# Gathering the small products of several streams in bursts, and FoX's stages at another place, in a one-core hybrid RWKV-7/FoX decoder block

## The chip, the cores and the metric

The kernel runs on one core of a Trainium2 chip. The core has a matrix engine (TensorE; PE in the profile, its weight loads PEld), a vector engine (VectorE, DVE), a scalar engine (ScalarE, ACT), GpSimd (POOL) and SyncE (SP), whose queue issues nearly all transfers. Each engine works through its own instructions in the order in which they were written for it, and waits on semaphores for the others. The metric is the time of one execution on the device in microseconds; the median of three runs is used.

## The reference

One decoder block over 16 meta tokens and 256 tokens (272 columns), width 2048, in float32. What is computed, cut to what matters:

```python
xn = _rms(h, n1)
z_rwkv, z_fox, z_gate = jnp.split(xn @ w_in, ...)          # 6608 + 4096 columns of w_in
z_rwkv = z_rwkv + (z_prev - z_rwkv) * mu                   # token shift
y_a = _rwkv7(z_rwkv, ...)    # scan over tokens: S = S*w + (S a) b + v k ; y = S r, 16 heads of 64
y_b = _fox(z_fox, ...)       # causal softmax attention with a forget bias, 16 heads of 64
merged = sigmoid(g_a) * (y_a @ w_a) + sigmoid(g_b) * (y_b @ w_b)
h = h + merged @ w_o
gate, up = jnp.split(_rms(h, n2) @ w_gu, 2, axis=-1)
out = h + (silu(gate) * up) @ w_dn
```

## The kernel before

**Weight products.** Every weight matrix streams through SBUF in blocks of 128x1024 (`wload`, L313 to L318): SP requests `raw`, ACT rounds it to `wh`, DVE forms the rest `wl = raw - wh`, three buffers of each. A job (`cm_jobs`) is one block: 24 products of about 260 columns (k, v, r, most of f), or 16 products for f's queries and the gates zg, alternating 512 and 256 columns. They are in a float32 form that PE takes in one pass, and they are the bulk of PE's work.

**Streams.** The RWKV and FoX work is done in four groups of four heads. For each group the weight products k, v, r, then f (queries, keys, values) are followed by gate jobs zg. What comes after a projection is written as Python generators ("streams"): `rwkv_bg` (the RWKV part of a group), `sums`/`norms` and `fox_bg` (FoX), `forget_gate`, `lerp`'s second half. Each piece of a stream up to a `yield` is a stage; a stage mostly has some small fp32 products on PE (`pe_mm`, L350), or transposes (`pe_tr`, L354), and reads of their results by ACT and DVE. The value that it yields is the least distance to its next stage, in ns.

**What sets the order.** PE's order is the order in which the program is written. `slot(ns)` is called after each few weight products; it adds their length to a clock, and if stages are due, it writes the one with the earliest due time there, and then lets `max(GAP, MIX * cost)` of weight products go by. So each stage stands alone between two weight products. The order on the other engines, and of SP's requests, is set by the framework's own scheduler.

**Names.** In `rwkv_bg`: ss (head sums of squares), kx (spreading a norm back), mat and mat0 (the matrices of a chunk of 64 tokens), bs (bonus), trbk, trv, tr (transposes), then the triangular solve on DVE (lt, lx; the "lane"), whose result goes out and comes back as X through requests on SP (d, X), then per chunk rhs, then u and y, then s and y, and at the end yT. QT and X (32x32 products) belong to the solve. In FoX: fss, fx, pv and pvm (values transposed), and per pair of heads m = 0, 1: bias (one buffer, requested on SP from ncd), sc (scores), the softmax on DVE and ACT, ppt and ptm (transposes of the probabilities), pT and pM (their copies by ACT), po (the product with the values).

**Shapes.** PE is used as 128x128 by the weight products, the transposes, ss and fss; as 128x64 by rhs, s, the second part of y, and po; as 64x64 by u and the first part of y; as 64x128 by mat and sc; as 32x32 by QT and X. Results of stages go to four auxiliary PSUM banks in turn (`aux_ps`); the other four belong to the weight products.

Of the kernel before, what the change touches and what calls it, by code (L numbers as in the profile page):

```python
# [12 lines left out]
AF = mybir.ActivationFunctionType  # L13
# [49 lines left out]
LANE = 24000  # L63
GAP = 250
LERP = 2800
BIAS = 7000
STEP = 1000
# [7 lines left out]
X_DIV = 2600  # L75
X_PT = 1400
Y_SQ = 1400
# [7 lines left out]
Y_TRBK = 1400  # L85
Y_TRV = 1100
Y_TR0 = 1600
# [9 lines left out]
def hybrid_block(ctx, tc, A, out, dbg=None):  # L97
# [240 lines left out]

    def spawn(gen, delay):
        streams.append([clock[0] + delay, gen])  # L340

    def stage(st):
        try:
            st[0] = clock[0] + (next(st[1]) or HOP)
        except StopIteration:
            streams.remove(st)

    def pe_mm(out_, lhsT, rhs, start, stop, skip=False):
# [7 lines left out]
    def slot(ns):  # L356


        clock[0] += ns
        if clock[0] < clock[1]:  # L360
            return
        due = [st for st in streams if st[0] <= clock[0]]
        if due:
            clock[2] = 0.0
            stage(min(due, key=lambda st: st[0]))
            clock[1] = clock[0] + max(GAP, MIX * clock[2])

# [285 lines left out]
    def rwkv_bg(g, box):  # L653
# [15 lines left out]
        nc.scalar.activation(sq, kk, AF.Square)  # L669
        yield Y_SQ  # L670
        kn_ = rw.tile([P, 12], F32, tag="kn", name=f"kn{g}", bufs=2)
# [4 lines left out]
        backs = [spread(kr_, m, L, f"kx{g}{m}") for m in range(2)]  # L676
        yield Y_SPREAD
        for m in range(2):
# [37 lines left out]
        split(*parts, sq[:, :, :T])  # L716
        yield Y_AB

# [3 lines left out]
        for m in range(2):  # L722
            pss = [aux_ps(f"mat{g}{m}{h}") for h in range(2)]
            for c in range(4):
                for h in range(2):
                    pe_mm(pss[h][:, c * P:(c + 1) * P], bk[hb(h), m, c].rearrange("p x t -> p (x t)"),
                                     ar[hb(h), :, m, tok(c)], start=True, stop=True)
            for h in range(2):
                nc.vector.tensor_tensor(NK[:, h, 4 * m:4 * m + 4, :], pss[h].rearrange("p (c w) -> p c w", w=P),
                                        bcast(mup, 4), op=ALU.mult)  # L730
            yield Y_MAT
        pss = [aux_ps(f"mat0{g}{h}") for h in range(2)]
# [32 lines left out]
        yield Y_NEXT  # L765

        bo = ot(f"bo{g}")
        for m in range(2):
# [5 lines left out]
            nc.gpsimd.tensor_scalar(bo[:, m, :], bo[:, m, :], vi("gn_b", m), None, op0=ALU.add)  # L774
        yield Y_BONUS

# [5 lines left out]
        for m in range(2):  # L782
            ps = aux_ps(f"trbk{g}{m}")
            for c in range(4):
                pe_tr(ps[:, c * P:(c + 1) * P], bkf[:, 4 * m + c, :], ident)
            nc.scalar.activation(BK[:, :, 4 * m:4 * m + 4, :].rearrange("p h c d -> p c h d"),
                                 ps.rearrange("p (c h d) -> p c h d", h=2, d=HD), AF.Copy)
            yield Y_TRBK
        ps = aux_ps(f"trv{g}")
# [47 lines left out]
        def step(c, S, BK, SV, NK, X, Y):  # L837
# [24 lines left out]
            for h in range(2):  # L862
                nc.vector.tensor_copy(SV[0:nt, h, mine, :], pv2(ps)[h * HD:h * HD + nt])
            yield Y_U
            if not last:
# [20 lines left out]
            if not first:  # L886
                nc.scalar.activation(Y.rearrange("p (m c) v -> p m c v", m=2)[:, :, c, :], pv2(psy), AF.Copy)
            yield HOP

# [7 lines left out]
        next(meta_steps)  # L897
        yield Y_XT
        ps = aux_ps(f"QT{g}")
# [6 lines left out]
        next(meta_steps)  # L906
        yield Y_QT
        ps = aux_ps(f"X12{g}")
# [22 lines left out]
        nc.vector.tensor_tensor(Y, Y, s2.unsqueeze(2).to_broadcast([P, 8, HD]), op=ALU.mult)  # L931
        yield NORM
        ps = aux_ps(f"yT{g}")
# [28 lines left out]
    def fox_jobs(g):  # L962
# [18 lines left out]
        def norms():  # L981
            while len(done) < 2:
                yield
            yield from rsqrt_steps(fx, hr, hs, [P, 20], "ht")
            yield X_RS

            nc.vector.tensor_tensor(hs[:, 0:8], hs[:, 0:8], hr[:, 0:8], op=ALU.mult)
            backs = [spread(hr[:, 8:20], m, L, f"fx{g}{m}") for m in range(2)]
            yield X_SPREAD
            for m in range(2):  # L990
                nc.vector.tensor_tensor(kn[:, m, :], kn[:, m, :], backs[m](), op=ALU.mult)
            yield
            ready.append(1)

        def post(dst, n):
            def f(pss):
                sqs = []
                for m in range(2):
                    ps = pss[m]
                    if dst is vv:  # L1000
                        nc.scalar.activation(dst[:, m, :], ps[:, :n], AF.Copy)
                        continue
                    sq = fx.tile([P, L], F32, tag="sqf", name=f"sqf{g}", bufs=3)
                    if dst is qn:
                        halves(dst[:, m, :], ps)
                        nc.scalar.activation(sq[:, :n], dst[:, m, :], AF.Square)
                    else:
                        nc.scalar.activation(sq[:, :n], ps[:, :n], AF.Square)
                        nc.scalar.activation(dst[:, m, :], ps[:, :n], AF.Copy, scale=qk8)
                    sqs.append(sq)  # L1010
                if dst is vv:
                    spawn(fox_bg(g, qn, kn, vv, hs, hr, ready), HOP)
                else:
                    spawn(sums(sqs, dst, n), SUMS)
                    if dst is kn:
                        spawn(norms(), PREP)
            return f
# [4 lines left out]
    def fox_bg(g, qn, kn, vv, hs, hr, ready):  # L1022
# [18 lines left out]
        cmb = cmask.unsqueeze(1).to_broadcast([P, 2, P])  # L1041
        for m in range(2):

# [9 lines left out]
            nc.gpsimd.tensor_tensor(bias[:, :, d1], bias[:, :, d1], cmb, op=ALU.add)  # L1053
            yield BIAS
            sums = fx.tile([P, 4], F32, tag="sums", name=f"sums{g}{m}", bufs=2)

            nq = [NMETA + P, L]
            cq_ = [slice(0, nq[0]), slice(nq[0], nq[0] + nq[1])]
# [5 lines left out]
            for t in range(2):  # L1064
                n = nq[t]
                for h in range(2):
# [7 lines left out]
                    nc.scalar.activation(s[:, :n], s[:, :n], AF.Exp, scale=r, bias=nm,  # L1074
                                         accum_out=sums[:, 2 * t + h:2 * t + h + 1])
            yield X_SC + X_EXP
# [18 lines left out]
            nc.scalar.activation(pM[:NMETA], ptm[:NMETA, :2 * P].rearrange("p (h q) -> p h q", h=2)[:, :, 96:], AF.Copy)  # L1095
# [12 lines left out]
            nc.scalar.activation(yb[:, 2 * g + m, :], po[:, :T], AF.Copy)  # L1108
            yield

# [262 lines left out]
```

## Time and profile before

| | before |
|---|---|
| median of 3 runs | 1564.14 us (1563.58 to 1564.69) |
| profiled execution | 1564.61 us |
| its span, first to last instruction | 1562.9 us |
| PE busy in the span | 1554.3 us, 99% |
| DVE, ACT, POOL busy | 1016.3, 766.8, 103.5 us |
| share of PE in the chain that ended last | 95% |
| weight transfers and all others | 283.33 MB, mean 181 GB/s |

The stages stand in the first 607 us of the span; after that come the last gate jobs, the branches, w_o, the FFN. A row of the timeline gives the start and length in us, the engine and line, the operation, the tile written and those read, the array shape and the operand's columns, and how many instructions were merged; a bracket at the end says how long the engine was idle before it and what ended that. Matmuls overlap, so their lengths add up to more than the time; it is the distance from start to start that counts. An fp32 product shows as two matmul rows, so four products are x8.

### The profile page before, as it was taken

What the parts mean: (1) busy time and instruction counts of PE and PEld (TensorE: products, weight loads), DVE (VectorE), ACT (ScalarE), POOL (GpSimd) and SP (SyncE); (2) the same over time, 40 slices, a digit from 0 to 9 for tenths busy, and PEclk for the clock granted to TensorE, in tenths of its full rate; (3) what the DMA queues carried; (4) which work ended last, traced back from release to release, by engine and by line L of the source; (5) the groups of instructions that cost most, each with busy time, mean ns of one, the idle gap of its engine ahead of it and who ended that gap; (6) DMA issues with size and microseconds to landing.
All of it is one profiled execution on the core that took longest, in us unless ns stands there. A gap on an engine that the chain in (4) does not pass through costs nothing.

```text
span 1562.9 us, 26174 instructions
## 1 busy us (share of the span) xinstructions
PE 1554.3 (99%) x10227; PEld 1366.6 (87%) x10227; DVE 1016.3 (65%) x1854; ACT 766.8 (49%) x1117; POOL 103.5 (7%) x194
## 2 busy tenths in 40 slices
PE   9999999999999999999999999999999999999998
PEld 8999988989889888999888888888888888888887
DVE  8878688677768856875655666566566656444443
ACT  6655455465445544654444554454445544333332
POOL 2121103102203100000000000000000000000000
PEclk9999999999999999999999999999999999999999
DMA  7656546546545566776666666666666666666664
GB/s 238 177 155 173 158 125 180 157 119 168 166 137 146 166 179 190 248 226 225 190 183 181 186 186 190 189 188 188 189 189 188 185 193 187 187 203 198 188 200 131
DMA packets 211483, 283.33 MB, mean 181 GB/s; under 512 B 23888, under 2 KB 128352, under 8 KB 211360
## 3 DMA queue, kind: packets, MB, share of 16 engines
q1 hardware_dynamic: 206752, 277.43, 60.3%
q10 hardware_dynamic: 4608, 4.23, 0.8%
q8 instruction: 80, 1.31, 0.4%
q14 instruction: 43, 0.35, 0.1%
HBM read 274.43 MB, written 7.19 MB: 180 GB/s over the span
## 4 chain that ended last, share of the span: by engine, by line
PE 95%; DVE 2%; DMA 1%; issue 1%; ACT 1%; SPq 0%; ACTq 0%; DVEq 0%; POOL 0%
PE up L387 10%; PE gt L387 10%; PE zg L387 7%; PE dn L1238 5%; PE dn L1237 5%; PE dn L1236 5%; PE up L389 5%; PE gt L389 5%; PE zg L389 3%; PE f L328 2%; PE f L387 2%; PE f L330 2%; PE f L329 2%; PE br L329 2%; PE br L330 2%; PE br L328 2%
## 5 line engine op out<-in xcount | busy, mean ns | idle before, releaser
L318 DVE TENSOR_TENSOR wl<-raw,wh 128x1024 fp32r<-128x1024 f32 (+1 forms) x496 | 605.2, 1221 | 438.7 <-ACT wh L317 437.7
L317 ACT ACTIVATE wh<-raw 128x1024 fp32r<-128x1024 f32 (+1 forms) x496 | 521.3, 1052 | 628.7 <-PE dn L1237 146.3
L387 PE MATMUL gt<-hts,wh 128*128 128x512 f32 x704 | 245.0, 394 | 0.0
L387 PE MATMUL up<-hts,wh 128*128 128x512 f32 x704 | 244.9, 394 | 0.0
L389 PE MATMUL gt<-hts,wl 128*128 128x256 f32 x660 | 186.2, 282 | 0.0
L389 PE MATMUL up<-hts,wl 128*128 128x256 f32 x660 | 186.0, 282 | 0.0
L387 PE MATMUL zg<-xhl,wh 128*128 128x512 f32 x512 | 184.3, 403 | 0.0
L387 PEld LDWEIGHTS up<-hts,wh 128*128 128x128 f32 x704 | 130.1, 188 | 26.5
L387 PEld LDWEIGHTS gt<-hts,wh 128*128 128x128 f32 x704 | 130.1, 188 | 26.4
L1237 PE MATMUL dn<-wh,acl 128*128 128x512 f32 x352 | 139.5, 396 | 0.0
L1236 PE MATMUL dn<-wh,ach 128*128 128x512 f32 x352 | 139.5, 396 | 0.0
L1238 PE MATMUL dn<-wl,ach 128*128 128x512 f32 x352 | 139.5, 396 | 0.0
L389 PE MATMUL zg<-xhl,wl 128*128 128x256 f32 x480 | 135.0, 281 | 0.0
L389 PEld LDWEIGHTS up<-hts,wl 128*128 128x128 f32 x660 | 124.7, 189 | 1.8
L389 PEld LDWEIGHTS gt<-hts,wl 128*128 128x128 f32 x660 | 124.7, 189 | 1.8
L387 PEld LDWEIGHTS zg<-xhl,wh 128*128 128x128 f32 x512 | 94.6, 188 | 20.9 <-issue 1.8
L389 PEld LDWEIGHTS zg<-xhl,wl 128*128 128x128 f32 x480 | 90.6, 189 | 1.1
L1238 PEld LDWEIGHTS dn<-wl,ach 128*128 128x128 f32 x352 | 66.3, 188 | 16.2
L1237 PEld LDWEIGHTS dn<-wh,acl 128*128 128x128 f32 x352 | 66.3, 188 | 16.2
L1236 PEld LDWEIGHTS dn<-wh,ach 128*128 128x128 f32 x352 | 66.3, 188 | 16.1
L328 PE MATMUL f<-xhl,wh 128*128 128x272 f32 x256 | 77.7, 303 | 0.0
L330 PE MATMUL f<-xhl,wl 128*128 128x272 f32 x256 | 73.8, 288 | 0.0
(452 smaller groups left out, 2783.3 us busy)
## 6 DMA issues: line engine op xcount, KB each, us to landing
raw<-in_w_gate_up_dram SPq DMA_DIRECT2D x176, 512.0 KB, 3.8
raw<-in_w_in_dram SPq DMA_DIRECT2D x160, 512.0 KB, 4.1
raw<-in_w_down_dram SPq DMA_DIRECT2D x88, 512.0 KB, 4.7
raw<-in_w_o_dram SPq DMA_DIRECT2D x32, 512.0 KB, 4.3
raw<-in_w_branch_a_dram SPq DMA_DIRECT2D x16, 512.0 KB, 4.4
raw<-in_w_branch_b_dram SPq DMA_DIRECT2D x16, 512.0 KB, 4.8
zgd<-zg ACTq DMA_DIRECT2D x30, 128.0 KB, 2.4
gate<-zgd SPq DMA_DIRECT2D x15, 256.0 KB, 5.6
```

What stands on the lines that cost most here:

```text
L317: nc.scalar.activation(wh[:prow, cs_], raw[:prow, cs_], AF.Copy)
L318: nc.vector.tensor_tensor(wl[:prow, cs_], raw[:prow, cs_], wh[:prow, cs_].bitcast(F32), op=ALU.subtract)
L328: nc.tensor.matmul(ps, wh, ah, start=first, stop=False)
L329: nc.tensor.matmul(ps, wh, al, start=False, stop=False)
L330: nc.tensor.matmul(ps, wl, ah, start=False, stop=last)
L387: nc.tensor.matmul(ps.rearrange("p (a t) -> p a t", a=2), wh, act, start=first, stop=last)
L389: nc.tensor.matmul(ps[:, :T], wl, act[:, 0, :], start=False, stop=False)
L1236: nc.tensor.matmul(box[t], ah[:, kt, ts_], wh[:, k, :], start=first, stop=False)
L1237: nc.tensor.matmul(box[t], al[:, kt, ts_], wh[:, k, :], start=False, stop=False)
L1238: nc.tensor.matmul(box[t], ah[:, kt, ts_], wl[:, k, :], start=False, stop=last)
```

## The change

`spawn` and the yields get a second number: how many auxiliary banks the next stage takes (0: a stage without products of this kind). `slot` sorts the due stages by due time. A due stage without banks is still written alone. Otherwise it takes all due stages, in that order, as long as their banks fit in the four, and writes them one behind the other. If only one is due, and another will be within `HOLD` (2000 ns) of its due time and would fit, it waits. Then the distances: `BIAS` 7000 to 28000, so that FoX's first scores come later; `X_PT` 1400 to 2000 and a new `X_PT0` of 4400. In `fox_bg` the work is rearranged: bias for m = 1 is requested and formed after the scores of m = 0 are reduced, and the scores of m = 1 are written in one stage with po of m = 0. The transposes ptm move into the fourth part of ppt's bank (no bank of their own), so there are two copies pM per pair instead of one. In `rwkv_bg` the two trbk stages become one, and trv and tr become one.

```diff
+HOLD = 2000
-BIAS = 7000
+BIAS = 28000
-X_PT = 1400
+X_PT = 2000
+X_PT0 = 4400
-Y_TRV = 1100
...
-    def spawn(gen, delay):
-        streams.append([clock[0] + delay, gen])
+    def spawn(gen, delay, banks=0):
+        streams.append([clock[0] + delay, gen, banks])
...
+        step, st[2] = step if isinstance(step, tuple) else (step, 0)
+        st[0] = clock[0] + step
...
         if clock[0] < clock[1]:
             return
-        due = [st for st in streams if st[0] <= clock[0]]
-        if due:
+        due = sorted((st for st in streams if st[0] <= clock[0]), key=lambda st: st[0])
+        group = [st for st in due if not st[2]][:1]
+        if due and not group:
+            banks = 0
+            for st in due:
+                if banks + st[2] <= 8 - PSM:
+                    group.append(st)
+                    banks += st[2]
+            if (len(group) == 1 and clock[0] < due[0][0] + HOLD and
+                    any(st[2] and st[0] > clock[0] and st[0] < due[0][0] + HOLD and banks + st[2] <= 8 - PSM
+                        for st in streams)):
+                return
+        if group:
             clock[2] = 0.0
-            stage(min(due, key=lambda st: st[0]))
+            for st in group:
+                stage(st)
             clock[1] = clock[0] + max(GAP, MIX * clock[2])
...
-        yield Y_SQ
+        yield Y_SQ, 1
...
-            yield Y_TRBK
+        yield Y_TRBK, 2
...
-        yield Y_TRV
...
-        yield LANE
+        yield LANE, 1
...
-            yield Y_RHS
+            yield Y_RHS, 2
...
-        for m in range(2):
+        def biases(m):
...
+        bs = biases(0)
+        yield BIAS, 2
+        sums = scores(0, *bs)
+        for m in range(2):
             yield X_SC + X_EXP
             nc.vector.reciprocal(sums, sums)
...
-            yield X_DIV
-            ptm = aux_ps(f"ptm{g}{m}")
+            if m == 0:
+                bs = biases(1)
+            yield X_DIV, 2
             pts = []
             for h in range(2):
                 ppt = aux_ps(f"ppt{g}{m}{h}")
+                pe_tr(ppt[:NMETA, 3 * P:], sc_t[h, 1][:, 2 * P:L], ident)
...
-                pe_tr(ptm[:NMETA, h * P:(h + 1) * P], sc_t[h, 1][:, 2 * P:L], ident)
                 pT = fx.tile([P, 416], F32, tag="pT", name=f"pT{g}{m}{h}", bufs=2)
                 nc.scalar.activation(pT, ppt[:, :416], AF.Copy)
+                nc.scalar.activation(pM[:NMETA, h, :], ppt[:NMETA, 480:], AF.Copy)
                 pts.append(pT)
-            yield X_PT
+            yield (X_PT, 1) if m else (X_PT0, 3)
             po = aux_ps(f"po{g}{m}")
...
+            if m == 0:
+                sums = scores(1, *bs)
             nc.scalar.activation(yb[:, 2 * g + m, :], po[:, :T], AF.Copy)
-            yield
```

On PE, in the first group, before: po of m = 1 (numbers are the program's own) stands alone between weight products of v; the scores and rhs stand in the same way elsewhere.

```order
L330 MATMUL v_1_2113<-xhl,wl 128x272
L350 MATMUL po_2256<-pT_2220,vt_1647 64x256
L350 MATMUL po_2256<-pT_2228,vt_1647 64x256
L350 MATMUL po_2256<-pT_2220,vt_1647 64x160
L350 MATMUL po_2256<-pT_2228,vt_1647 64x160
L350 MATMUL po_2256<-pM,vm 64x32 x2
L328 MATMUL v_0_2112<-xhl,wh 128x272
```

On PE at the same part of the program, after: po of m = 0, the scores of m = 1 and the next chunk's rhs, between weight products of r.

```order
L332 MATMUL r_1_2275<-xhl,wl 128x258
L355 MATMUL po_2354<-pT_2205,vt_1629 64x256
L355 MATMUL po_2354<-pT_2214,vt_1629 64x256
L355 MATMUL po_2354<-pT_2205,vt_1629 64x160
L355 MATMUL po_2354<-pT_2214,vt_1629 64x160
L355 MATMUL po_2354<-pM,vm 64x32 x2
L355 MATMUL sc_2362<-kn_994,qn_993 128x144
L355 MATMUL sc_2363<-kn_994,qn_993 128x144
L355 MATMUL sc_2362<-kn_994,qn_993 128x272
L355 MATMUL sc_2363<-kn_994,qn_993 128x272
L355 MATMUL rhs_2386<-sv_1613,NK_1377 64x64 x4
L330 MATMUL r_1_2275<-xhl,wh 128x258
```

Three stages of two streams, each with its own shape, now follow each other with no weight product between.

On PE at the transposes ahead of the first group's solve, before: the first half of trbk alone (the second half, and FoX's pvm and pv, stand further down in the same way).

```order
L330 MATMUL f_0_1372<-xhl,wl 128x272
L354 MATMUL trbk_1559<-ident,bk_1277 128x128 x4
L328 MATMUL f_1_1373<-xhl,wh 128x272
L329 MATMUL f_1_1373<-xhl,wh 128x272
L330 MATMUL f_1_1373<-xhl,wl 128x272
```

The same transposes on PE, after.

```order
L407 MATMUL zg_0_1563<-xhl,wl 128x256
L359 MATMUL trbk_1617<-ident,bk_1286 128x128 x4
L359 MATMUL trbk_1623<-ident,bk_1286 128x128 x4
L359 MATMUL pvm_1631<-ident,vv_995 16x128
L359 MATMUL pv_1630<-ident,vv_995 128x128 x2
L359 MATMUL pvm_1631<-ident,vv_995 16x128
L359 MATMUL pv_1630<-ident,vv_995 128x128 x2
L405 MATMUL zg_0_1563<-xhl,wh 128x512
```

Three stages of transposes that stood apart are one burst of fourteen.

On SP, the requests after the first group's solve, before: the solve's results out (d) and back (X), then weights, then a bias.

```order
L826 DMA d_1475<-lx_1665 16x1x32 x4
L830 DMA X_1667<-d_1474 32x8x32 x3
L831 DMA X_1668<-d_1475 16x2x32
L830 DMA X_1667<-d_1474 32x8x32
L831 DMA X_1668<-d_1475 16x2x32
L313 DMA raw<-in_w_in_dram 128x4x256 x3
L1047 DMA bias_3371<-ncd 128x544
```

The same requests on SP, after.

```order
L843 DMA d_1510<-lx_1692 16x1x32 x4
L847 DMA X_1694<-d_1509 32x8x32 x3
L848 DMA X_1695<-d_1510 16x2x32
L847 DMA X_1694<-d_1509 32x8x32
L848 DMA X_1695<-d_1510 16x2x32
L1065 DMA bias_2150<-ncd 128x544
L315 DMA raw<-in_w_in_dram 128x4x256 x4
```

The bias request of the second half of the same group stands directly behind the read-backs and ahead of the weights; it does so in the third group too. In the second and fourth group three and two weight requests go first. In the first and third group, 12 weight requests instead of 11 stand between the solve's inputs and its results.

## Rows read from the trace of the kernel before

**Rows 1.** The page: span, and busy us of each engine with its share
```profile
span 1562.9 us, 26174 instructions
PE 1554.3 (99%) x10227; PEld 1366.6 (87%) x10227; DVE 1016.3 (65%) x1854; ACT 766.8 (49%) x1117; POOL 103.5 (7%) x194
```
**Rows 2.** Timeline of PE around one rhs stage: start us, length us, instruction
```profile
305.02 0.29 PE L328 MATMUL r<-xhl,wh 128*128 128x258 f32 x1
305.14 0.29 PE L329 MATMUL r<-xhl,wh 128*128 128x258 f32 x1
305.27 0.28 PE L330 MATMUL r<-xhl,wl 128*128 128x258 f32 x1
305.48 0.45 PE L350 MATMUL rhs<-sv,NK 128*64 128x64 f32 x8
305.86 0.39 PE L328 MATMUL r<-xhl,wh 128*128 128x258 f32 x1
306.08 0.28 PE L329 MATMUL r<-xhl,wh 128*128 128x258 f32 x1
```
**Rows 3.** The same view at the next stage, u and y
```profile
307.87 0.45 PE L350 MATMUL u<-R,X 64*64 64x64 f32 x8
308.15 0.40 PE L350 MATMUL y<-S1-1_4007,ar 64*64 64x64 f32 x8
308.48 0.39 PE L328 MATMUL r<-xhl,wh 128*128 128x258 f32 x1
```
**Rows 4.** The same view where X and s stand together
```profile
300.07 0.29 PE L330 MATMUL v<-xhl,wl 128*128 128x272 f32 x1
300.29 0.69 PE L350 MATMUL X<-X,QT 32*32 32x32 f32 x32
300.91 0.45 PE L350 MATMUL s1-1_4002<-SV,BK 128*64 128x64 f32 x8
```
**Rows 5.** The same view at a trbk stage, and inside a ppt burst
```profile
240.50 0.29 PE L330 MATMUL f<-xhl,wl 128*128 128x272 f32 x1
240.62 0.60 PE L354 MATMUL trbk<-ident,bk 128*128 128x128 f32 x4
...
241.19 0.29 PE L329 MATMUL f<-xhl,wh 128*128 128x272 f32 x1
...
141.66 0.60 PE L354 MATMUL ppt<-ident,s 128*128 128x128 f32 x4
142.09 0.27 PE L354 MATMUL ptm<-ident,s 128*16 128x128 f32 x1
```
**Rows 6.** The same view where fss begins
```profile
212.66 0.29 PE L330 MATMUL f<-xhl,wl 128*128 128x272 f32 x1
212.79 0.95 PE L350 MATMUL fss<-bsum,sqf 128*128 128x2 f32 x8
```
**Rows 7.** The same view, third group's solve: stages before which PE stood
```profile
394.63 0.44 PE L354 MATMUL ppt<-ident,s 128*128 128x128 f32 x2 [0.30 <-DVE s L1081]
...
421.50 1.05 PE L350 MATMUL po<-pT,vt 128*64 128x256 f32 x6 [1.47 <-ACT pT L1093]
```
**Rows 8.** Timeline of ACT just before that po
```profile
419.98 1.06 ACT L317 ACTIVATE wh<-raw 128x1024 fp32r<-128x1024 f32 x1 [5.04 <-DMA raw<-in_w_in_dram]
```
**Rows 9.** Timeline of DVE, first group: first and last step of scores, and a split
```profile
159.07 0.30 DVE L1070 CUSTOM_DVE_ANT_0 s<-sc,b 128x144 f32<-128x144 f32 x1
...
160.49 0.33 DVE L1073 TENSOR_SCALAR nm<-nm,hr 128x1 f32<-128x1 f32 x2
...
166.24 1.23 DVE L318 TENSOR_TENSOR wl<-raw,wh 128x1024 fp32r<-128x1024 f32 x1 [2.88 <-ACT wh L317]
```
**Rows 10.** Timeline of SP's queue: the first group's last read-back and what follows
```profile
160.51 0.45 SPq L831 DMA_DIRECT2D X<-d  x1
161.00 1.52 SPq L313 DMA_DIRECT2D raw<-in_w_in_dram  x3
```
**Rows 11.** Timeline of PE: the first product of the block split at 166.24
```profile
169.46 0.39 PE L328 MATMUL v<-xhl,wh 128*128 128x272 f32 x1
```

More of the change, by code (lines that the diff above doesn't have):

```diff
@@ L337, in hybrid_block @@
     clock = [0.0, 0.0, 0.0]
-    def spawn(gen, delay):
-        streams.append([clock[0] + delay, gen])
+    def spawn(gen, delay, banks=0):
+        streams.append([clock[0] + delay, gen, banks])
     def stage(st):
         try:
-            st[0] = clock[0] + (next(st[1]) or HOP)
+            step = next(st[1]) or HOP
         except StopIteration:
             streams.remove(st)
+            return
+        step, st[2] = step if isinstance(step, tuple) else (step, 0)
+        st[0] = clock[0] + step
     def pe_mm(out_, lhsT, rhs, start, stop, skip=False):
@@ L361, in slot @@
             return
-        due = [st for st in streams if st[0] <= clock[0]]
-        if due:
+        due = sorted((st for st in streams if st[0] <= clock[0]), key=lambda st: st[0])
[9 more added lines that the diff above has]
+                        for st in streams)):
+                return
+        if group:
             clock[2] = 0.0
-            stage(min(due, key=lambda st: st[0]))
+            for st in group:
+                stage(st)
             clock[1] = clock[0] + max(GAP, MIX * clock[2])
@@ L676, in rwkv_bg @@
         backs = [spread(kr_, m, L, f"kx{g}{m}") for m in range(2)]
-        yield Y_SPREAD
+        yield Y_SPREAD, 2
         for m in range(2):
@@ L716, in rwkv_bg @@
         split(*parts, sq[:, :, :T])
-        yield Y_AB
+        yield Y_AB, 2
         NK = nkt(f"NK{g}")
@@ L730, in rwkv_bg @@
                                         bcast(mup, 4), op=ALU.mult)
-            yield Y_MAT
+            yield Y_MAT, 2
         pss = [aux_ps(f"mat0{g}{h}") for h in range(2)]
@@ L764, in rwkv_bg @@
                                       ar[hb(h), 0, m, NMETA:].rearrange("p (c t) -> p c t", t=HD))
-        yield Y_NEXT
+        yield Y_NEXT, 2
         bo = ot(f"bo{g}")
@@ L774, in rwkv_bg @@
             nc.gpsimd.tensor_scalar(bo[:, m, :], bo[:, m, :], vi("gn_b", m), None, op0=ALU.add)
-        yield Y_BONUS
+        yield Y_BONUS, 2
         BK, SV = (bst(t, f"{t}{g}") for t in ("bt", "sv"))
@@ L863, in step @@
                 nc.vector.tensor_copy(SV[0:nt, h, mine, :], pv2(ps)[h * HD:h * HD + nt])
-            yield Y_U
+            yield Y_U, 2
             if not last:
@@ L887, in step @@
                 nc.scalar.activation(Y.rearrange("p (m c) v -> p m c v", m=2)[:, :, c, :], pv2(psy), AF.Copy)
-            yield HOP
+            yield (HOP, 0) if last else (HOP, 1)
         S = [None]
@@ L897, in rwkv_bg @@
         next(meta_steps)
-        yield Y_XT
+        yield Y_XT, 2
         ps = aux_ps(f"QT{g}")
@@ L906, in rwkv_bg @@
         next(meta_steps)
-        yield Y_QT
+        yield Y_QT, 2
         ps = aux_ps(f"X12{g}")
@@ L931, in rwkv_bg @@
         nc.vector.tensor_tensor(Y, Y, s2.unsqueeze(2).to_broadcast([P, 8, HD]), op=ALU.mult)
-        yield NORM
+        yield NORM, 1
         ps = aux_ps(f"yT{g}")
@@ L988, in norms @@
             backs = [spread(hr[:, 8:20], m, L, f"fx{g}{m}") for m in range(2)]
-            yield X_SPREAD
+            yield X_SPREAD, 2
             for m in range(2):
@@ L1011, in f @@
                 if dst is vv:
-                    spawn(fox_bg(g, qn, kn, vv, hs, hr, ready), HOP)
+                    spawn(fox_bg(g, qn, kn, vv, hs, hr, ready), HOP, 2)
                 else:
-                    spawn(sums(sqs, dst, n), SUMS)
+                    spawn(sums(sqs, dst, n), SUMS, 1)
                     if dst is kn:
@@ L1053, in fox_bg, with scores @@
             nc.gpsimd.tensor_tensor(bias[:, :, d1], bias[:, :, d1], cmb, op=ALU.add)
-            yield BIAS
+            return b1, bias
+        nq = [NMETA + P, L]
+        def scores(m, b1, bias):
             sums = fx.tile([P, 4], F32, tag="sums", name=f"sums{g}{m}", bufs=2)
-            nq = [NMETA + P, L]
             cq_ = [slice(0, nq[0]), slice(nq[0], nq[0] + nq[1])]
@@ L1075, in fox_bg @@
                                          accum_out=sums[:, 2 * t + h:2 * t + h + 1])
+            return sums
+        bs = biases(0)
+        yield BIAS, 2
+        sums = scores(0, *bs)
+        for m in range(2):
             yield X_SC + X_EXP
@@ L1088, in fox_bg @@
                 ppt = aux_ps(f"ppt{g}{m}{h}")
+                pe_tr(ppt[:NMETA, 3 * P:], sc_t[h, 1][:, 2 * P:L], ident)
                 for c, t, k in ((T - 96, 0, 1), (0, 0, 0), (P, 1, 0), (T + 32, 1, 1)):
                     pe_tr(ppt[:, c:c + P], sc_t[h, t][:, k * P:(k + 1) * P], ident)
-                pe_tr(ptm[:NMETA, h * P:(h + 1) * P], sc_t[h, 1][:, 2 * P:L], ident)
                 pT = fx.tile([P, 416], F32, tag="pT", name=f"pT{g}{m}{h}", bufs=2)
                 nc.scalar.activation(pT, ppt[:, :416], AF.Copy)
+                nc.scalar.activation(pM[:NMETA, h, :], ppt[:NMETA, 480:], AF.Copy)
                 pts.append(pT)
-            nc.scalar.activation(pM[:NMETA], ptm[:NMETA, :2 * P].rearrange("p (h q) -> p h q", h=2)[:, :, 96:], AF.Copy)
-            yield X_PT
+            yield (X_PT, 1) if m else (X_PT0, 3)
             po = aux_ps(f"po{g}{m}")
```

## The prediction

> **What bounds the kernel now.** Read the page's busy times first [rows 1]: TensorE (PE) is busy for 1554.3 of a span of 1562.9 us, VectorE (DVE) for 1016.3 and ScalarE (ACT) for 766.8. The chain that ended last is PE for 95%. So a microsecond is won only where PE has a microsecond less to do or to wait. The change touches nothing of the weight products; it moves the small fp32 products of the RWKV and FoX streams ("stages") that are slipped in between them. The second view is therefore PE's own instructions in order of time around such stages, and what counts there is the step from one start to the next: in the steady stream (305.02, 305.14, 305.27) [rows 2] a weight product of some 260 columns starts .12 to .13 us after the one before; I use .12.
>
> **What one stage costs PE, and what of it goes away in company.**
> A stage of four 64-column products (rhs) [rows 2]: the weight product at 305.27 should have been followed at 305.39; rhs starts at 305.48, .09 late. From rhs's start to the next weight product are .38 us, and that one is followed only .22 later instead of .12. In all 306.08 - 305.27 less two steps of .12, .57 us. The stage of u and y holds eight products of that size [rows 3], and from its start to the next weight product are .61 instead of .38: four more products cost .23. So of rhs's .57 only .23 is work, and .34 is paid for going out of the weight stream and back: .09 on the way in, .10 for the slow step of the first weight product, and .15 between, of which I give .09 to the way out (from rhs's last start, 305.48 + .45 - .22 = 305.71, .15 pass to the weight product at 305.86; two products that run side by side take .06).
>
> What is saved if two such stages stand together is read from a pair that the kernel before has already [rows 4]: X (32x32 products) and s (64-column ones) with no weight product between. X's sixteen pairs start from 300.29 to 300.79 (300.29 + .69 - .19), .03 apart, and s starts at 300.91, .12 later: .09 more than a step, the same .09 that a stage pays on its way in from the weight stream. So between stages of different shape the second still pays its way in, and the first saves the way out and the slow weight product: .09 + .10 = **.19 us for each such place**. Two stages of the same shape would save all .34.
>
> Full-width stages behave otherwise. Four transposes of trbk [rows 5] take 241.19 - 240.50 less two steps of .125, .44 us, and four transposes in the middle of the ppt burst take 142.09 - 141.66 = .43. All of it is work: transposes standing alone pay nothing for it, and **gathering them saves nothing**. The products with a 2-column operand (ss, fss) also start without delay, .13 after the weight product [rows 6]; gathered with a tiled stage I give them the slow weight step alone, .10, between 0 and .19.
>
> The Trainium skill ("TensorEngine Tiling (Array Packing)", Key Properties) says that changing the tiling mode, not just the tile, drains the engine. The trace agrees in that rhs and X pay and trbk doesn't; by the rule alone po, sc and rhs together would have four changes of mode instead of six, which saves two thirds of what the change seems to promise on such a group at most.
>
> Now the count. In the program's order PE has 141 bursts of stages before and 88 after, with the same 941 small and 8574 other products. The 53 places at which a stage now follows another:
> - 15 of tiled stages of different shape (sc to rhs 6, po to sc 4, y to po 3, y to mat 2): 15 x .19 = 2.85 us;
> - 1 of the same shape (po to s): .34;
> - 9 of ss or fss before a tiled stage (fss to mat 3, fss to s 2, ss to s 2, fss to u, ss to u): 9 x .10 = .9;
> - 7 of a tiled stage before a full-width one (y to kx 2, rhs to ppt 2, rhs to kx, mat to fss, kx to fss): the slow weight step goes, but the full-width stage loses the head start of its weights; half, 7 x .05 = .35;
> - 21 of transposes before whatever follows (ppt to rhs 6, yT to mat 1, and 14 among transposes): 0.
> Together **4.4 us**. Bounds: 1.6 if the 15 save nothing, 10.9 if the first 32 places all save .34.
>
> **What the later FoX stages do.** Before, FoX's scores, softmax and ppt stand in the triangular solve ("lane"), where DVE works through 62 dependent little operations; now they stand beside the RWKV chain (rhs, u, s). In the lane PE waited for FoX: a ppt transpose for DVE's softmax by .30 [rows 7], with a second like it in the last group, and po for ACT's copy pT by 1.47, because ACT stood for 5.04 us on a weight transfer ahead of it [rows 7, 8]. Now po comes 20 weight products or more behind ppt instead of 10 to 15, so these 2.1 us go. Added work: eight more small copies (pM) on ACT, which is idle half of the time; nothing on DVE, POOL, SP or PE. Cost 0, unless ACT becomes late.
>
> The wait that the change itself adds (a lone stage may stand back by up to HOLD, 2 us of counted weight time) costs PE nothing, since weight products go on meanwhile; it could lengthen the streams past the weight work that covers them. It doesn't: the last stage, yT of the last group, stands behind 3364 weight products instead of 3374.
>
> New waits. Four bursts are po, sc and rhs: all four auxiliary banks. The u and y behind them need po's and sc's banks. DVE's reduction of the scores lasts from 159.07 to 160.8 [rows 9], 1.75 us, and a 1.23 us weight split may stand ahead of it: 1.75 to 3.0 us after sc. The next burst starts after rhs (.5) and 15 weight products (15 x .12 = 1.8; in the last group 12 gate products, half of them twice as wide, about 12 x .18 = 2.2), 2.3 to 2.7 us after sc. So 0 to .7 each, 0 to 2.8 in all; R behind the pT copies on ACT and the later chain can add a few tenths. I take 1.0; 0 to 5 are the bounds. A negative one is already in the 2.1.
>
> **Sum.** 4.4 + 2.1 - 1.0 = 5.5 us less. The profiled execution took 1564.61 us for its span of 1562.9 and would be at 1559.1; the median of the runs is 1564.14, .47 lower, so **1558.6 us**, 0.35% faster. (A measurement here tells about 0.2%, 3.1 us, from no change.)
>
> **Rivals.**
> A, every tiled or 2-column stage saves its whole .34 as the number of bursts suggests: 32 x .34 = 10.9, 1564.1 - 10.9 - 1.1 = 1552.1. For it: nothing but the analogy with stages of one shape. Against it: the .09 between X and s.
> B, a change between two shapes costs as much as going back to the weight stream (X and s were a lucky pair, 64x128 scores before 128x64 rhs a worse one): the 2.85 go, 1564.1 - 1.6 - 1.1 = 1561.4. Such a pair does not occur in the trace.
> C, PE waits in the long bursts take the gain: three or four banks are held until DVE and ACT have read them, and the chain R, u, s now queues behind FoX's exps and copies. At the bound of 5 us: 1564.1 - 4.4 - 2.1 + 5 = 1562.6.
> D, slower: on SP's queue. In groups 0 and 2 the bias request of FoX's second half now stands directly behind the solve's last read-back and ahead of any weight request; before, the weight requests followed at once (read-back at 160.51, weights at 161.00) [rows 10]. The bias buffer is single, so SP stands until the first scores are reduced. The first weights of 161.00 were split until 166.24 + 1.23 = 167.47 and used at 169.46 [rows 9, 11]: 2.0 us to spare, and one more job (24 steps of .12, 2.9 us) now goes ahead of the solve's requests. A stand of w costs w - 4.9 in each of two lanes; from w = 9.2 it is 3.1 us slower than before. At w = 12: 1564.1 - 5.5 + 14 = 1573. Against it: the scores stand 48 weight products ahead of rhs, and their reduction takes 1.75 us.
>
> **How the numbers follow.** The forecast has .55, A .10, B .14, C .14, D .07. The range 1554 to 1563 holds the forecast, B and most of C; A, D and the end of C are outside, about .2. Faster by over 0.2% (below 1561.0): forecast .52, A .10, B .06, together .68. Within 0.2%: .03 + .08 + .12 = .23. Slower: .02 of C and D, .09.
>
> **What would show it.** Right: sc to rhs and po to sc start .09 us above a step apart; transposes step by .11 in any company; the sum of what the bursts take falls by 4 to 5 us, and po no longer waits for pT. Wrong: a burst with starts .3 apart where shapes change (B) or with no gap (A); waits of u, y or ppt for DVE or ACT in PE's list (C); weight products that wait for DVE after the lane (D).

## The result

The changed kernel takes 1569.22 us (1567.95 to 1569.84) against 1564.69 (1563.58 to 1565.88): ratio 1.0029 [1.0019, 1.0039]. It is **slower by 4.5 us, 0.3%**; 1558.6 was forecast, and the range ended at 1563. The profiled execution has a span of 1567.7 us (before 1562.9).

The page of after, against [rows 1]: the span, and the busy time of each engine.

```profile
span 1567.7 us, 26153 instructions
PE 1553.1 (99%) x10227; PEld 1368.0 (87%) x10227; DVE 1017.2 (65%) x1854; ACT 764.3 (49%) x1125; POOL 99.2 (6%) x194
```

PE has 1.2 us less to do in 4.8 us more time; it stands more. Its waits by cause (what waited, for whom, us in all, times, longest):

```profile
PE tr L359 <- ACT sv L813: 2.6, 2, 1.3
PE fx L359 <- ACT bt L804: 1.4, 2, 0.7
...
PE zg L405 <- ACT wh L319: 1.1, 1, 1.1
PE zg L407 <- DVE wl L320: 1.0, 1, 1.0
PE X L355 <- ACT QT L922: 0.9, 4, 0.4
PE r L332 <- DVE wl L320: 0.7, 2, 0.5
```

None of these is in the trace of before, and the waits that it had at po and ppt [rows 7] are gone.

**The saving is there.** A burst's cost is taken as in the prediction: from the last weight product ahead of it to the second one behind it, less two usual steps. PE's timeline at po, sc and rhs in one burst:

```profile
180.67 0.28 PE L332 MATMUL r<-xhl,wl 128*128 128x258 f32 x1
180.88 0.92 PE L355 MATMUL po<-pT,vt 128*64 128x256 f32 x8
181.63 0.26 PE L355 MATMUL po<-pM,vm 128*64 128x32 f32 x4
181.82 0.97 PE L355 MATMUL sc<-kn,qn 64*128 64x144 f32 x8
182.72 0.45 PE L355 MATMUL rhs<-sv,NK 128*64 128x64 f32 x8
183.10 0.39 PE L330 MATMUL r<-xhl,wh 128*128 128x258 f32 x1
183.33 0.29 PE L331 MATMUL r<-xhl,wh 128*128 128x258 f32 x1
```

183.33 - 180.67 less .24 is 2.42. Before, po and sc alone stood so, here between gate products, of which two steps take .35:

```profile
526.21 0.28 PE L389 MATMUL zg<-xhl,wl 128*128 128x256 f32 x1
526.41 0.92 PE L350 MATMUL po<-pT,vt 128*64 128x256 f32 x8
...
527.69 0.28 PE L389 MATMUL zg<-xhl,wl 128*128 128x256 f32 x1
...
538.55 0.28 PE L389 MATMUL zg<-xhl,wl 128*128 128x256 f32 x1
538.75 0.97 PE L350 MATMUL sc<-kn,qn 64*128 64x144 f32 x8
...
539.99 0.28 PE L389 MATMUL zg<-xhl,wl 128*128 128x256 f32 x1
```

With rhs as in [rows 2] the three apart cost 1.13 + 1.09 + .57 = 2.79. Summed over all clean bursts (those in which nothing waited) after saves 4.55 us.

**It is given back inside the bursts.** All bursts together cost 122.4 us, those of before 122.25, of which 3.27 were the old waits. (The trace has 89 bursts in after and 144 in before, so 55 places merge: the prediction's 53 leave out bs before fx, twice, which saves nothing.) So 8.1 us of new waits stand in after, each the excess over the parts alone: 3.0 at yT + trv + tr (two bursts of 2.82 for parts of 1.31), 1.8 at trbk + fx (two of 2.88 for 1.98), 2.5 at X + s (1.72 to 2.19 three times for 1.20, against [rows 4]), .5 at QT, .2 at mat.

X waits for ACT's copy of QT (L922). On ACT, in the first group of after, that copy stands behind FoX's copies pT and two weight roundings; in before (last row) ACT stood idle for it:

```profile
173.12 0.49 ACT L1122 ACTIVATE pT<-ppt 128x416 f32<-128x416 f32 x1
...
173.59 1.04 ACT L319 ACTIVATE wh<-raw 128x1024 fp32r<-128x1024 f32 x1
174.66 0.78 ACT L922 ACTIVATE QT<-QT 32x256 f32<-32x256 f32 x2
...
171.54 0.78 ACT L905 ACTIVATE QT<-QT 32x256 f32<-32x256 f32 x2 [1.57 <-PE QT L350]
```

It is the same in the third group, and in the second FoX's exps stand there (to 298.1, QT's copy at 298.13).

**And weights came late.** PE, first group's solve:

```profile
129.47 0.39 PE L405 MATMUL zg<-xhl,wh 128*128 128x512 f32 x1
130.98 0.51 PE L405 MATMUL zg<-xhl,wh 128*128 128x512 f32 x1 [1.12 <-ACT wh L319]
132.45 0.38 PE L407 MATMUL zg<-xhl,wl 128*128 128x256 f32 x1 [0.96 <-DVE wl L320]
...
133.20 0.63 PE L405 MATMUL zg<-xhl,wh 128*128 128x512 f32 x1
...
133.84 0.63 PE L405 MATMUL zg<-xhl,wh 128*128 128x512 f32 x1
```

The steps from 129.47 and from 130.98 are 1.28 and 1.24 us too long. Then a pair of products takes .64 us (133.20 to 133.84) instead of .35, for 2.6 us. The windows (busy us of PE, PEld, DVE, ACT and POOL, then granted clock, DMA share and GB/s) say why: the clock was granted at half, 1.2 instead of 2.4 GHz, after PE had stood:

```profile
127.00:129.00 2.00, 2.00 (x13) 1.74 (x12) 0.03 (x1) 0.38 (x1) 0.00 (x0) 1.00 0.00 0
129.00:133.00 4.00, 1.92 (x10) 1.14 (x9) 3.76 (x14) 3.13 (x4) 0.00 (x0) 0.97 0.10 33
133.00:136.00 3.00, 3.00 (x11) 2.62 (x10) 2.93 (x7) 0.09 (x1) 0.00 (x0) 0.50 0.81 214
```

The granted clock of before is 1.00 in all of these. With about 1.6 us for the slow stretch this place costs 4.1, and .39 and .61 are lost to late weights, with no fall of the clock, at 173 and 428. The account: - 4.55 - 3.27 + 8.1 + 4.1 + 1.0 = + 5.4; the span is 4.8 longer, and I have not found the .6 between.

### The profile page after: what moved, and what is told of

The parts are those of the page before. It is cut to its first block, busy times and chain, and to the rows that moved or that the text cites. A ratio compares the mean times of both kernels' runs of the same rounds, so it can differ in the third digit from the quotient of the medians.

```text
span 1567.7 us, 26153 instructions
## 1 busy us (share of the span) xinstructions
PE 1553.1 (99%) x10227; PEld 1368.0 (87%) x10227; DVE 1017.2 (65%) x1854; ACT 764.3 (49%) x1125; POOL 99.2 (6%) x194
## 3 DMA queue, kind: packets, MB, share of 16 engines
q8 instruction: 80, 1.31, 0.3%
## 4 chain that ended last, share of the span: by engine, by line
PE 92%; DVE 3%; DMA 2%; ACT 2%; issue 1%; SPq 0%; POOL 0%; ACTq 0%; DVEq 0%
PE up L405 10%; PE gt L405 10%; PE zg L405 7%; PE dn L1269 5%; PE dn L1268 5%; PE dn L1267 5%; PE up L407 5%; PE gt L407 5%; PE zg L407 3%; PE f L330 2%; PE f L405 2%; PE br L331 2%; PE br L330 2%; PE br L332 2%; PE f L331 2%; PE f L332 2%
```

## Experiments

Line numbers are those of each run's own kernel. "Waits" are PE's, read from the distance of starts; each ratio is to the kernel before on the same chip.

**1. The banks.** In the second and fourth group tr waits for ACT's read of trv (sv, L813) in the same burst, and fx for that of trbk (bt, L804): they were given the same auxiliary banks. The reason is on DVE, which reads bs (written by PE at 242.35 to 242.98) only at 253.56:

```profile
252.64 0.88 DVE L963 SCALAR_TENSOR_TENSOR ya<-ya,vcol,bo 128x256 f32<-128x256 f32 x2 [0.67 <-ACT ya L959]
253.56 0.76 DVE L791 TENSOR_TENSOR bo<-bs,v 128x256 f32<-128x256 f32 x2
```

bo and gg share three buffers, and none is free until the group before has ended. Before, that was at 238.61 and bo followed at 240.31; now yT stands 52 weight products later. Meanwhile bs holds two of the four banks.

```diff
-        return rw.tile([P, 2, T], F32, tag="o", name=name, bufs=3)
+        return rw.tile([P, 2, T], F32, tag="o", name=name, bufs=4)
...
-                    sq = fx.tile([P, L], F32, tag="sqf", name=f"sqf{g}", bufs=3)
+                    sq = fx.tile([P, L], F32, tag="sqf", name=f"sqf{g}", bufs=2)
```

A buffer of FoX's squares is given up for the room. No run changes that alone; in this one no fss waits for it.

> One more buffer for bo and gg (tag o, 4 instead of 3; a third buffer of FoX's squares is given up for the room). PE's order is that of the changed kernel, instruction by instruction. Theory 1 (banks): in the changed kernel DVE's read of bs in the second and fourth group stands until the group before has ended, since bo finds no buffer; bs holds two of the four auxiliary banks, and trbk with fx, and trv with tr, must take the same two after one another inside one burst (PE stood 2 x 1.28 before tr and 2 x 0.68 before fx; the four bursts are 4.8 us over the sum of their parts). With the buffer these four go: 1569.2 - 4.8 = 1564.4. Theory 2 (FoX's new place beside the chain loads ACT and DVE, and PE waits for them wherever it stands): the wait moves on to the next stage or weight split, 1568 to 1570.

1564.89 us, 1.0007 [0.9998, 1.0016]. The bursts fall from 122.4 to 117.4 us. PE and DVE, where tr and bo stand now:

```profile
250.28 0.60 PE L359 MATMUL trv<-ident,v 128*128 128x128 f32 x4
250.72 0.27 PE L359 MATMUL tr<-ident,bk 128*128 128x128 f32 x1
```
```profile
243.44 0.76 DVE L791 TENSOR_TENSOR bo<-bs,v 128x256 f32<-128x256 f32 x2 [0.70 <-PE bs L790]
```

tr follows trv by .44 as a transpose does; the wait moved nowhere. Shown: the banks that bs holds for want of a buffer cost 4.5 us by the profiled spans (1567.7 and 1563.2), 3.4 by the two ratios.

**2. No groups, and FoX back in the lane.**

```diff
-            for st in due:
-                if banks + st[2] <= 8 - PSM:
...
+            group = due[:1]
+            if 0 and (len(group) == 1 and clock[0] < due[0][0] + HOLD and
...
```

> The changed kernel with one stage for each burst again (no group, no standing back); FoX's new place and the gathered trbk and trv/tr stay, and po with the scores of m = 1, which are one stage now. Theory 1: a burst alone finds other banks, so the 4.8 us of tr and fx go, and the saving of the junctions goes but for po to sc (4.5 - 0.8 = 3.7): 1569.2 - 4.8 + 3.7 = 1568.1, with no wait over 0.5 us before tr or fx. Theory 2 (FoX's place costs): the waits stay and the junctions are lost, about 1573.

1568.67 us, 1.0032 [1.0022, 1.0043]: the number of theory 1 for another reason. tr and fx don't wait, and the late weights at 130 are gone too, but yT waits 5.2 us, and one s 1.6:

```profile
PE yT L359 <- DVE Y L945: 3.5, 2, 1.8
...
PE yT L359 <- DVE hr L259: 1.1, 1, 1.1
```

The other half: FoX's code and BIAS of before, groups kept.

> The changed kernel with FoX's scores, ppt and po back in the lane, as the kernel before has them (wait of 7000, a bank for ptm, no po with sc); groups and gathered transposes stay. 37 places merge instead of 55. Theory 1: about two thirds of the 4.5 us of saving (3.0), one pair of bursts in which a bank comes twice (about 3 us, half of what the changed kernel has and a little more), po's old wait of 1.5 back: near the kernel before, 1564 to 1566. Theory 2 (FoX's place is what costs): 1564.7 - 3.0 = 1561.7, and the waits before tr and fx are small.

1570.32 us, 1.0037 [1.0024, 1.0049]: neither theory. The bursts cost 122.2 us as before (waits of 2.0 at ppt, 1.3 at po, 1.3 at fx and trv, .5 at yT), and the weights are late at 129.7 by the same 1.27 + 1.25 us, and once more at 516.7 by 1.5. So the late weights come with the groups, not with FoX's place.

**3. The late weights.** ACT and then DVE in after, around the fault:

```profile
118.96 1.06 ACT L319 ACTIVATE wh<-raw 128x1024 fp32r<-128x1024 f32 x1 [2.99 <-PE zg L405]
...
128.55 0.38 ACT L411 ACTIVATE zg<-zg 128x256 f32<-128x256 f32 x1 [3.04 <-PE zg L405]
129.42 0.35 ACTq L1169 DMA_DIRECT2D zgd<-zg  x1
129.87 1.06 ACT L319 ACTIVATE wh<-raw 128x1024 fp32r<-128x1024 f32 x1 [0.94 <-DVE lt L834]
```
```profile
122.47 0.19 DVE L834 TENSOR_TENSOR lt<-lx,ln 112x29 f32<-112x29 f32 x1
128.97 0.42 DVE L412 TENSOR_TENSOR zg<-zg,zg 128x256 f32<-128x256 f32 x1 [6.30 <-ACT zg L411]
...
131.18 1.22 DVE L320 TENSOR_TENSOR wl<-raw,wh 128x1024 fp32r<-128x1024 f32 x1
```

The same rows of ACT and DVE in before:

```profile
124.53 1.06 ACT L317 ACTIVATE wh<-raw 128x1024 fp32r<-128x1024 f32 x1 [0.45 <-PE zg L387]
128.91 0.38 ACT L393 ACTIVATE zg<-zg 128x256 f32<-128x256 f32 x1 [3.32 <-PE zg L387]
```
```profile
126.87 1.22 DVE L318 TENSOR_TENSOR wl<-raw,wh 128x1024 fp32r<-128x1024 f32 x1
129.33 0.42 DVE L394 TENSOR_TENSOR zg<-zg,zg 128x256 f32<-128x256 f32 x1 [1.09 <-ACT zg L393]
```

Two fixed orders have turned. ACT has the gate's copy zg and its store ahead of the next block's rounding wh, and stands 3.0 us for PE, which ends that gate at 128.5; before, that rounding came first. DVE has the gate's sum zg behind the third step of the solve, stands 6.3 us, and then does the next steps of the solve one behind the other until the next split at 131.18; before, zg stands behind the seventh step and the split. The rounding ends at 130.93 and gives PE's first gap (its product starts at 130.98), the split ends at 132.40 and gives the second (132.45). Both orders turned in each of the six kernels whose weights are late at 130, and neither in the other eleven; no run turns one alone, so it is not shown that mending DVE's order would have been enough.

With `HOLD` the first mat waits for fss, so mat0 stands at weight product 715 instead of 691, the solve comes later, and the scheduler, which orders ACT and DVE, put zg ahead on both. The kernel before with only this delay:

```diff
-Y_AB = 4400
+Y_AB = 6900
```

> The kernel before with one number changed: mat comes 2.5 us of counted time later behind its products (6900 instead of 4400), so that the first mat stands at weight product 658 and mat0 at 712, where the changed kernel has them (658 and 715; before 634 and 691). Nothing is grouped and FoX stays in the lane. Theory 1 (weights late in the lane): in the changed kernel mat stands back for fss6, all of the solve comes 3 us later, and DVE's fixed order then has the gate's sum zg behind the third step of the solve instead of the seventh or later, ahead of the next weight split; DVE stood 6.3 us for it and PE 1.28 + 1.24 us for weights at 129.5 to 132.7, with a granted clock of 0.50 behind that: 4.2 us in all. In this kernel DVE has zg at the third step or sooner in all four solves, so at least the first loses about 4 us: 1568.3, and up to 1580 if all four do. Rival (the wait comes from the group itself, three stages of transposes in a row at 119.6): no gap over 1 us at 130, 1564 to 1565.

1573.23 us, 1.0057 [1.0045, 1.0070]. PE and DVE:

```profile
130.26 0.39 PE L387 MATMUL zg<-xhl,wh 128*128 128x512 f32 x1
131.76 0.50 PE L387 MATMUL zg<-xhl,wh 128*128 128x512 f32 x1 [1.11 <-ACT wh L317]
133.24 0.51 PE L389 MATMUL zg<-xhl,wl 128*128 128x256 f32 x1 [0.98 <-DVE wl L318]
```
```profile
129.76 0.42 DVE L394 TENSOR_TENSOR zg<-zg,zg 128x256 f32<-128x256 f32 x1 [5.90 <-ACT zg L393]
```

The gaps are those of after to .02 us, with nothing grouped, and ACT's rounding is behind zg here too. The other three solves lost little for it (.5 at most); the bursts cost 5 us more, 4.1 at y and 2.8 at ppt, with po's 1.9 gone. The cure, with the fourth buffer: mat's first stage is not grouped.

```diff
-        yield Y_AB, 2
+        yield Y_AB
```

> The kernel with the fourth buffer, and mat's first stage neither grouped nor standing back; all else as it is. PE loses two merged places, mat0 stands at weight product 700 instead of 715, and DVE has zg at the seventh step of every solve. Theory 1: no wait for weights at 130 and no fall of the clock: 1564.9 - 4.2 = 1560.7, 0.2% faster than the kernel before. Rival (the weights are late because FoX's second bias request stands ahead of them on SP, or because 9 weight products are still too late): 1563 to 1565.

1562.71 us, 0.9988 [0.9979, 0.9997]; no gap at 130, and ACT's rounding is ahead of zg again (126.84 and 129.52). It missed 1560.7 by 2 us: the waits at X and QT rose to 4.2, and 1.03 stand before a weight product at 170. Without any standing back:

```diff
-HOLD = 2000
+HOLD = 0
```

> The kernel with the fourth buffer, and no standing back (HOLD 0): stages are grouped only where they are due together, 20 places instead of 55; mat0 stands at weight product 691 as before. Theory 1: the weights' wait at 130 goes (4.2), some two thirds of the junctions' saving go (3.0), and yT, which stands at weight product 1336 as in the kernel with one stage for each burst (where it waited 5.2 us for DVE in three places), waits again: 1564.9 - 4.2 + 3.0 + 5.2 = 1568.9; without that wait 1563.7. Rival (standing back costs nothing and gives all of the saving): 1564.9 + 3 = 1568 with the wait at 130 still there.

1569.73 us, 1.0033 [1.0021, 1.0046], as expected: mat0 in time, but yT waits 6.1 us.

**4. Moving the chain by a little.** With the fourth buffer, and then with mat ungrouped as well, X was put later behind QT.

```diff
-Y_QT = 1200
+Y_QT = 2200
```

> The kernel with the fourth buffer, and X 1 us later behind QT (2200 instead of 1200 of counted time). In the changed kernel PE stands before X's second pair for ACT's copy QT (0.9 us in four places, with the slow steps around them 2.5 us in three bursts over the 1.20 that X and s take without a wait). Theory 1: another 2.5 us less than with the buffer alone, 1562. Rival: the chain behind X comes later and meets FoX's work in another way, so the waits come back at s, u or rhs: 1564 or more.

> As the one above, and X 0.5 us later behind QT (1700 instead of 1200). The kernel with the fourth buffer still loses 2.2 us at X (it waits for ACT's copy QT). Theory 1: 1 to 2 us of these go, 1559 to 1560, if the later chain meets no other wait; DVE has zg at the seventh step or later in all solves, so no weight wait over 1 us. Rival (each shift of the chain opens another wait of the same size, as with X 1 us later, where mat stood 3.4 us for DVE and a weight split 2 us): 1562 or more.

With 2200 it took 1569.99 us, 1.0035 [1.0022, 1.0048], and with 1700 and mat ungrouped 1566.0, 1.0010 [1.0001, 1.0019]: the rival both times. X's waits went in the first and sank to .9 in the second; instead mat waited for DVE (3.5 and 2.3 us), and one weight product for its split (2.0 each, at 262 and 258).

**5. FoX's second bias and FoX's time**, each on the kernel of 1562.7. There SP's queue had, against [rows 10],

```profile
161.18 0.45 SPq L848 DMA_DIRECT2D X<-d  x1
162.15 0.34 SPq L1065 DMA_DIRECT2D bias<-ncd  x1
162.54 1.53 SPq L315 DMA_DIRECT2D raw<-in_w_in_dram  x3
```

First `bs = biases(1)` moves from the division to the stage of ppt:

```diff
-            if m == 0:
-                bs = biases(1)
             yield X_DIV, 2
...
+            if m == 0:
+                bs = biases(1)
             yield (X_PT, 1) if m else (X_PT0, 3)
```

> The kernel with the fourth buffer and mat's first stage ungrouped (1562.7), and the request for the second half's bias moved from the stage that divides the scores to the stage of ppt, some 48 weight products later; SP then has one or two weight requests between the solve's last read-back and that bias request in every group. Theory 1 (a bias request ahead of the weights holds SP: in the first group SP stood from 161.63 to 162.15 and the weights asked for after it were split at 168.4, and PE stood 1.03 + 0.39 us for weights at 170 and 423): these 1.4 us and the 0.2 before u go, 1561.1. Rival (the weights of that place are late whatever stands ahead, since the solve's own requests hold SP): 1562 to 1563.

1561.43 us, 0.9986 [0.9977, 0.9995]. The gaps before weight products go (1.03 and .39 to less than .3), but X waits 4.3 instead of 2.5. Then also `LANE` 24000 to 25200:

> As the one above, and the chain behind the solve 1.2 us of counted time later (LANE 25200). In the kernel at 1562.7 QT waits for the read-back's transpose XT and for its neighbours (1.7 us over 1.19 in three places) and X for ACT's QT (2.5 in two). Theory 1: QT's 1.7 go, some of X's too: 1558 to 1560. Rival (a chain that comes later only meets FoX's work elsewhere): 1561 to 1564 with new waits of the same size.

1559.68 us, 0.9971 [0.9961, 0.9982], as expected: only the first group's X and s (2.2) and u (.3) still wait. Instead of these two, FoX later:

```diff
-BIAS = 28000
+BIAS = 30500
```

> The kernel at 1562.7 with FoX's scores 2.5 us of counted time later (BIAS 30500): the second bias request stands behind one or two weight requests, as in the kernel with the moved request, by time instead of by place, and the scores' softmax falls behind the solve's read-back transpose. Theory 1: 1.4 us of weight waits go and QT no longer waits for the softmax; X may wait longer behind the exps: 1560 to 1562. Rival (new waits of the same size): 1562 to 1565.

**1556.84 us, 0.9956 [0.9943, 0.9968], faster than both kernels.** Its page (of the stages only one QT still waits, .5 us):

```profile
span 1555.2 us, 26165 instructions
PE 1548.2 (100%) x10227; PEld 1365.2 (88%) x10227; DVE 1015.3 (65%) x1854; ACT 765.3 (49%) x1125; POOL 99.3 (6%) x194
```
The bursts cost 114.8 us, 7.4 below before, and the span is 7.7 shorter. The last step was chosen for the bias and QT; that all waits at X went too was not forecast (1560 to 1562 was), so part of this gain is luck. On ACT the copy of QT now stands ahead of pT's (169.01 and 169.81 in the first group). The later time alone, on the changed kernel:

> The changed kernel with nothing but FoX's scores 2.5 us later (BIAS 30500); bo has three buffers, mat stands back for fss as it does in the changed kernel. By DVE's order zg stands at the third step of the solve in the first and the third group, and in four bursts a bank comes twice. Theory 1 (three separate causes): the waits at X (2.5) and for weights behind the bias (1.0) go, the tr and fx waits (4.8) and the weights' wait at 130 (4.2) stay: 1569.2 - 3.5 = 1565.7, and up to 4 more if the third group's weights come late too. Rival (FoX's time was the one cause): 1557 to 1560.

1574.06 us, 1.0062 [1.0049, 1.0076]. tr, fx and the weights at 130 wait exactly as in after, the third group's weights 1.3 more, and X, whose waits were expected to go, 5.5 instead of 2.5. So FoX's time was not the one cause, and the number missed theory 1 too.

**6. Does FoX's place cost by itself?** Without groups, first yT later (`NORM` 6000), then FoX later too, then with FoX's old time the chain later:

> The changed kernel with one stage for each burst (1568.7), and yT 1.8 us of counted time later (NORM 6000 instead of 4200). There yT stood 1.3, 2.0 and 2.0 us for DVE in three groups, and a second s and y pair 0.8. Theory 1 (FoX's new place costs nothing by itself, the loss is that of a stage that comes due before DVE is done): yT's 5.2 us go, 1563.5, 0.8 below the kernel before, of which the old waits at po and ppt (3.3) and po to sc (0.7) are more than that. Theory 2 (FoX's work beside the chain loads DVE, so what yT doesn't wait another stage will): 1566 to 1569.

> One stage for each burst, FoX beside the chain, with yT later (NORM 6000) and FoX's scores 2.5 us later (BIAS 30500): the timing of the best grouped kernel (1556.8) without its groups. Theory 1 (a stage that comes due before its input makes PE wait; FoX's place itself is free): the waits at QT (4.3 us over its parts), s and y (1.1) and yT go; against the kernel before the old waits at po and ppt (3.3) and po to sc (0.7) are gone: 1560 to 1561, and the groups are worth the remaining 4. Theory 2 (without groups FoX's work beside the chain always meets a wait): 1565 or more.

1569.62 us, 1.0038 [1.0026, 1.0051], and 1569.55, 1.0037 [1.0024, 1.0049]. Both fell to theory 2: yT is cured, and QT waits for the read-back instead (4.3 and 5.2 us over its parts), s 3.5 and 2.5, in the second also sc 2.0. But QT stood 20 to 36 weight products earlier than before in the runs without groups, as the gathered transposes leave two stages out ahead of the solve.

```diff
-LANE = 24000
+LANE = 27600
```

> One stage for each burst, FoX beside the chain at the changed kernel's time (BIAS 28000), yT later (NORM 6000), and the chain behind the solve 3.6 us of counted time later (LANE 27600): QT then stands at weight products 1038, 1713, 2385 and 3006, where the kernel before has it (1041, 1716, 2388, 3008); in the runs alone so far it stood 20 to 35 products earlier, since the gathered transposes leave two stages out ahead of the solve, and it waited 4 to 5 us for the read-back. Theory 1 (FoX's place is free, the chain came too early): no wait over 0.5 us at QT, s or yT; 1564.3 - 3.3 (old waits at po and ppt) - 0.7 (po to sc) = 1560.3, and the groups are worth the 3.5 from there to 1556.8. Theory 2 (FoX beside the chain without groups always meets a wait): 1565 or more.

1563.47 us, 0.9996 [0.9987, 1.0005]: between the theories. QT doesn't wait (1.20 with u in all four groups). The old waits of 3.3 are gone, and 2.1 at trbk and 1.3 at X and s have come. So with these distances FoX's place neither costs nor wins much alone; with those of the other three runs it cost 4 to 6 us. Whether the groups alone are worth the whole 6.6 us from here to 1556.8 stays open, since 3.4 of these are waits that another choice of distances might also remove.

## Why the prediction was wrong

- **What a junction saves** was right: 4.55 us against 4.4. po + sc + rhs saved .37 (.38 forecast), u y + po .19, po + s .31 (.34), transposes nothing, y + kx .05. Of the places of ss and fss (.10 forecast, .19 at most), fss + s and fss + u saved .10, ss + s and fss + mat .20 and .19. Rivals A and B fall. The Trainium skill ("TensorEngine Tiling (Array Packing)", Key Properties) names a drain at a change of mode; the trace agrees in that a stage behind another shape saved .19 and one behind its own .31. By that rule po, sc and rhs save two of the four changes of mode that the number of bursts promises, so half and not the prediction's two thirds; .37 of .68 is near that.
- **The old waits** went; with the slow restart behind them they were 3.3 us, not 2.1.
- **"New waits ... I take 1.0; 0 to 5"** is the first step that failed. I asked only for the banks behind po, sc and rhs; the u and y there waited 0. The waits came at stages that I had booked at 0: the transposes (4.8) and X (2.5), 8.1 in all. Rival C had the mechanism, but the wrong place and too low a price (it took 5). That bs would keep its banks could have been read before: bo's buffer is free only after yT of the group before, and the change moves yT by 52 weight products, from ahead of bs to behind it.
- **"Cost 0, unless ACT becomes late"**, for FoX's later stages, is part of it: ACT did become late. FoX's copies and exps stand ahead of QT's copy there, and X waited 2.5 us for it; in the run with FoX back in the lane X doesn't wait.
- **"The wait that the change itself adds ... costs PE nothing"** is the second step that failed: I looked at the last stage alone (3364 against 3374 products). mat0 moved by 24, and with it the orders on ACT and DVE turned; 4.1 us. I read PE's and SP's order of the new program, but not ACT's and DVE's, where the rows stood.
- **Rival D** was right as a mechanism and small: 1.0 us in the first and third group. Such gaps go in the run that moves the bias behind a weight request.

## What to carry over

Merging small products saves what the junctions cost, but each stage that is delayed or hurried for company takes its reads, its banks and its buffers along: count the banks that are still held, not those that the burst asks for, and ask which buffer the later end of one stream frees for the next. Compare the orders of all engines, not only of the one that the change is about: a gate's read that slipped ahead of the weights' rounding on ACT and their split on DVE cost 4.1 us, nearly the 4.4 that merging was to win. Chains with hand-set distances should be retuned after such a change; the same groups gave 1569 and 1557.

## What the hardware showed

After PE had stood 1.28 and 1.24 us within 3.2 us, the granted clock was 0.50 for the next 3 us (0.97 over the 4 us before, 0.95 over the 2 us behind), which added about 1.6 us to 2.5 of waiting; in five other kernels the same gaps at this place were followed by a clock of 0.50 to 0.56 too. After the single waits of 1.28 us before tr the weight products went on at their usual .35 a pair, with 1.00 granted. One stand of 1.84 us before a weight product (at 262, with the fourth buffer and X 1 us later) was followed by 0.53 from 266 to 269. A wait costs PE more than its bracket says: po's 1.47 [rows 7] were 1.94 by the distance of starts, and ppt's .30 were .67.
